# Three latent blocks opened at once with GpSimd's sums of squares put off, and the last retention head's result slots placed behind the sample states

## The chip, the core and the metric

The kernel runs on one core of one Trainium2 chip. A core has five engines with an instruction stream each: TensorE (PE) for matrix products, VectorE (DVE), ScalarE (ACT), GpSimd (POOL) and SyncE (SP), which here mainly issues DMA transfers. On-chip memory is SBUF; matmul results land in PSUM, which is held in banks of 128 x 512 floats. TensorE runs at 1.2 or at 2.4 GHz; the granted clock in the rows is the mean share of the higher level (0.5 is the lower one throughout). The metric is device time in microseconds for one execution; the median of the runs shown is taken.

## What is computed

One step of a decoder layer for a prompt of 512 tokens and, in the same pass, 8 samples of 4 tokens (32 columns), 544 columns in all. Cut from the reference:

```
u = rms_norm(x, p['norm_mix_pre'])
rq, rk, rv, rg, cq, ckv, kpe, xq, gates = split_cols(u @ p['w_in'])
o_ret, ret_state = ret_fn(rope(rq), rope(rk) * RET_DK ** -0.5, rv)    # 4 heads, chunks of 128
o_ret = silu(rg) * (o_ret * rsqrt(mean(o_ret ** 2) + eps));  a_ret = o_ret @ p['w_ret_o']
q = rms_norm(cq) @ p['w_uq'];  ckv = rms_norm(ckv);  kpe = rope(kpe)
a_mla = mla_fn(q, ckv, kpe) ...        # samples: softmax over 2048 paged past positions
a_x = mem_attend(xq, mem_k, mem_v) @ p['w_x_o']
g = sigmoid(gates)                     # 3 x 1024 columns
mixed = g[0] * a_ret + g[1] * a_mla + g[2] * a_x
h = x + rms_norm(mixed @ p['w_out']);  y = h + swiglu_ffn(rms_norm(h))
```

Beside y, the new latents, rotary keys, memory keys and the retention states of prompt (`ret_p`) and samples (`ret_s`) are outputs. The state of a sample is s = s0 * gamma + k v per head; its output takes the state before (s0) and the 4 new tokens.

## The kernel before

Everything is laid out with features on the partitions and the 544 columns along the free axis. A weight product of 128 output features is a *block*: `dense` (L215) goes over two halves of 272 columns and eight chunks k of 128 input features, and because fp32 is split into a high and a low part, it does three matmuls for each (L228 `uh` by `wh`, L229 `ul` by `wh`, L230 `uh` by `wl`): 48 matmuls a block. `uh` and `ul` are the high and low parts of x times the gain. Weights come by SyncE (L199) in tiles `wr`; ScalarE makes `wh` (L207), VectorE or, where it is told so, GpSimd makes `wl` (L208). A ring of 5 `wr`, 5 `wh` and 4 `wl` holds them.

*The start.* A loop over k (L329 to L349) loads x, makes `uh` (L334) and `ul` (L335) on VectorE, squares x on ScalarE (L337, L340) and adds the squares on GpSimd into `xs` (L341). The weights of the first latent blocks (`T_CQ`, `T_CQ+1`, `T_CQ+2`) are asked for in and behind that loop. `latent_project` (L402) then runs the blocks, each with an evacuation by ScalarE (L410, L411) and an add on GpSimd (L414). A block needs two PSUM banks; `mm_tile` hands out three in turn, and `sq_tile` three of another tag. `T_CQ` and `T_CQ+1` have their banks at once. `col_stats` sums `xs` over the features by matmuls with ones (L282, `st`), takes the reciprocal root on VectorE (L245 to L251) and spreads it over the partitions by matmuls (L299, `sb`) into `R1` (L303). `R1` scales each later evacuation of u @ w_in, the rotary ones included.

*Retention* (L659 to L758) runs four heads. Each projects q, k, v, turns them, takes chunk products, builds four chunk states (`pu` L715, `state` L718 and L720, the last stored as `ret_p` by SyncE L722) and outputs (`po` L732, L734), squares them on ScalarE, takes a reciprocal root and scales into `on` (L739), projects the swish gate (two `T_RG` blocks), transposes (`pt` L751) and splits into `oh` and `ol` (L753, L236). In the last head `sample_states` (L623) is called ahead of the chunk states: for four groups of two samples each it loads four states s0 (L634), multiplies them into `poS` (L639), forms key-value products (`km` on GpSimd L647, `puS` L651), updates the state on VectorE (L653) and stores it (L654). The states, the `oh`/`ol` results and gates all take slots of one pool of 41 (`slot`). The last head's `oh` and `ol` slots are taken at its start, three slots `gA` ahead of its chunk products. Then come gate blocks `T_G` and `T_G+1`, `pt`, and `T_G+2`.

*The paged stage* behind it reads pages of past keys and values, by SyncE (L892) and by indirect transfers of GpSimd (L895), for two groups of four samples: key scores `ps_sc` (L903, L910), then value sums `po` (L958) in eight steps a group. Between these, `deal` puts pieces of dense blocks from a list `units` (`w_ret_o` and the remaining gates) by shares worked out from the list's length.

What sets the order: each engine runs its instructions in the order of its own stream, which a tile scheduler made from the program's order and from due times; SyncE's queue blocks behind a transfer that waits. Slots and PSUM banks make later work wait until the earlier reader is done. `together` adds a wait of one instruction for others.

Of the kernel before, what the change touches and what calls it, by code (L numbers as in the profile page):

```python
# [9 lines left out]
F32R = mybir.dt.float32r  # L10
# [4 lines left out]
ALU = mybir.AluOpType  # L15
# [7 lines left out]
RH, DK, DV = 4, 128, 256  # L23
# [134 lines left out]
def step(ctx: ExitStack, tc: tile.TileContext, I, O):  # L158
# [35 lines left out]
    def f32(ap):  # L194
        return ap.bitcast(F32)
# [6 lines left out]
    def wload(src, n, lo=V):  # L202

        raw = wraw(src, n)
        wh = ring.tile([128, 512], F32R, tag="wh", name="wh", bufs=RB[1])[:, :n]
        wl = ring.tile([128, 512], F32R, tag="wl", name="wl", bufs=RB[2])[:, :n]
        S.copy(wh, raw)  # L207
        lo.tensor_tensor(wl, raw, f32(wh), op=ALU.subtract)  # L208
        return wh, wl

    def wk(src, lo=V):

        n = src.shape[1]
        return [(*wload(src[:, c:min(c + 512, n)], min(512, n - c), lo), 0, min(512, n - c) // 128) for c in range(0, n, 512)]
# [51 lines left out]
    def gain(c):  # L266
        return gains[:, c:c + 1]
# [43 lines left out]
    def slot(name, dt=F32):  # L311
        return big.tile([128, NT], dt, tag="big", name=name, bufs=41)
# [5 lines left out]
    def at_tile(name):  # L318
        return at.tile([128, 512], F32, tag="at", name=name, bufs=AB[0])

    def sq_tile(name):
        return at.tile([128, 512], F32, tag="sq", name=name, bufs=SQB[0])

    first = {}

    cqw = []
    uh, ul = [], []
    xs = slot("xs")
    for k in range(8):  # L329
        x = xp.tile([128, NT], F32, tag="x", name="x", bufs=8)  # L330
        SY.dma_start(x, I["xT"][128 * k:128 * k + 128, :])
        h = slot("uh", F32R)
        l = slot("ul", F32R)
        V.tensor_scalar(h, x, gain(G_PRE + k), None, op0=ALU.mult)  # L334
        V.scalar_tensor_tensor(l, x, gain(G_PRE + k), f32(h), op0=ALU.mult, op1=ALU.subtract)  # L335
        if k == 0:
            S.square(xs, x)  # L337
        else:
            sq = xp.tile([128, NT], F32, tag="sq", name="sq", bufs=7)
            S.square(sq, x)  # L340
            G.tensor_tensor(xs, xs, sq, op=ALU.add)  # L341
        uh.append(h)
        ul.append(l)
        if k < 2:
            cqw.append(wload(I["w_in"][T_CQ][:, 512 * k:512 * k + 512], 512))
            first[T_CQ] = [(*w, 0, 4) for w in cqw]
        if k == 3:
            first[T_CQ + 1] = wk(I["w_in"][T_CQ + 1], G)
    SY.dma_start(ident, I["ident"])  # L349
    first[T_CQ + 2] = wk(I["w_in"][T_CQ + 2], G)  # L350
    tabs = latp.tile([128, 2, NT], F32, tag="tabs", name="tabs")
    cosP, sinP = tabs[:, 0, :], tabs[:, 1, :]
    rtab = [slot("rtab") for _ in range(2)]
# [13 lines left out]
    def w_in(t, evac, ps=None):  # L367
        dense(first.pop(t) if t in first else wk(I["w_in"][t]), uh, ul, evac, ps=ps)
# [34 lines left out]
    def latent_project(t0, n):  # L403
        raw, ss = [], slot("lss")
        for i in range(n):
            r_ = slot("lraw")
            sq = ss if i == 0 else slot("lsq")

            def evac(p, s, e):
                S.copy(r_[:, s:e], p)  # L410
                S.square(sq[:, s:e], p)  # L411
            w_in(t0 + i, evac, [sq_tile("mm"), sq_tile("mm")] if t0 + i == T_CQ + 1 else None)
            if i:
                G.tensor_tensor(ss, ss, sq, op=ALU.add)  # L414
            raw.append(r_)
        return raw, ss
# [171 lines left out]
    def gate_evac(dst):  # L588
        def evac(p, s, e):
            z = tmp_tile("gz", "rp_a")[:, :e - s]  # L590
            V.tensor_tensor(z, p, R1[:, s:e], op=ALU.mult)
            S.activation(dst[:, s:e], z, AF.Tanh, scale=0.5)
        return evac

    gA = []
    SH = (1, 2)

    def step_(h):
# [23 lines left out]

    def sample_states():  # L623

        po = at_tile("poS")
        for h in range(RH):
            r = slice(32 * h, 32 * h + 32)
            PE.matmul(po[r, :DV], lhsT=sm[r], rhs=vtS[r], start=True, stop=False, tile_position=(32 * h, 32 * h))
        for b2 in range(DB // 2):
            o = slice(2 * DV * b2, 2 * DV * b2 + 2 * DV)  # L630
            ss, loads = [], []
            for h in range(RH):
                s0 = slot512("s0").rearrange("p (u e) -> p u e", u=2)
                loads.append(SY.dma_start(s0.rearrange("p u e -> p (u e)"), I["s0"][h][:, o]))  # L634
                ss.append(s0)
            for u in range(2):
                b = 2 * b2 + u
                for h in range(RH):
                    lead = PE.matmul(po[32 * h:32 * h + 32, :DV], lhsT=qm[:, h, 32 * b:32 * b + 32], rhs=ss[h][:, u, :],  # L639
                                     start=False, stop=b == DB - 1, tile_position=(0, 32 * h))  # L640
                    if u == 0 and h == 0:
                        together(lead, loads)
            for h in range(RH):
                km = kmp[h]
                if b2 % 2 == 0:
                    km = kmp[h] = slot512("km", F32R)[:96].rearrange("p (b d) -> p b d", b=4)
                    G.tensor_tensor(km, f32(kst[h]).unsqueeze(1).to_broadcast([96, 4, 128]),  # L647
                                    small[:96, C_BM + 2 * b2:C_BM + 2 * b2 + 4].unsqueeze(2).to_broadcast([96, 4, 128]), op=ALU.mult)
                pu = at_tile("puS").rearrange("p (u e) -> p u e", u=2)
                for u in range(2):  # L650
                    PE.matmul(pu[:, u, :], lhsT=km[:, (2 * b2 + u) % 4, :], rhs=vst[h], start=True, stop=True)  # L651
                s0 = ss[h]
                V.scalar_tensor_tensor(s0, s0, GAM4[h], pu, op0=ALU.mult, op1=ALU.add)  # L653
                SY.dma_start(O["ret_s"][h][:, o], s0.rearrange("p u e -> p (u e)"))  # L654
        S.copy(orS, po[:, :DV])
# [1 line left out]
    kmp = [None] * RH  # L657

    for h in range(RH):  # L659
        oh += [slot("oh", F32R) for _ in range(2)]  # L660
        ol += [slot("ol", F32R) for _ in range(2)]
        qT = retp.tile([128, NT], F32, tag="qT", name="qT", bufs=2)
        kT = retp.tile([128, NT], F32, tag="kT", name="kT", bufs=2)
        w_in(T_RQ + h, rope_evac(*rtab, 64, qT))
# [5 lines left out]
            step_(h)  # L670
        if h == 0:
            mstat = memory_prepare()
        if h == RH - 1:
            gA += [slot("gA") for _ in range(3)]


        pst = at_tile("pst").rearrange("p (c i) -> p c i", c=4)
# [26 lines left out]
        kst.append(retp.tile([96, 128], F32R, tag="kst", name="kst", bufs=4))  # L704
        vst.append(retp.tile([96, DV], F32R, tag="vst", name="vst", bufs=4))
        sample_keys(h, px, qT)
        if h == RH - 1:
            sample_states()

        states = []  # L710
        for c2 in range(2):
# [25 lines left out]
        rsqrt(ssq, 4, DV, rr, 4.0)  # L737
        for cc in range(4):
            V.tensor_scalar(on[:, cc, :], pos_[cc // 2][:, cc % 2, :], rr[:, cc:cc + 1], None, op0=ALU.mult)  # L739
        sg = [retp.tile([128, NT], F32, tag="sg", name="sg", bufs=2) for _ in range(2)]  # L740
        for e in range(2):
            w_in(T_RG + 2 * h + e, silu_evac(sg[e]))
# [10 lines left out]
            V.tensor_tensor(og, pt.rearrange("p c i -> p (c i)"), sg[e][:, :NP], op=ALU.mult)  # L753
            split(og, oh[2 * h + e][:, :NP], ol[2 * h + e][:, :NP])
        if h == RH - 1:
            w_in(T_G + 2, gate_evac(gA[2]))
        if h == 1:
            memory_kv(*mstat)  # L758

# [668 lines left out]
```

## Time and profile before

| | us |
|---|---|
| median of three runs | 1243.65 |
| lowest, highest | 1238.79, 1243.99 |
| the profiled execution | 1244.79 |
| its span, first to last instruction | 1243.0 |
| TensorE busy in it | 1184.3 (95%) |
| VectorE, ScalarE, GpSimd busy | 664.0, 450.2, 325.2 |
| mean granted clock | 0.981 |

The profile is one execution. A timeline row has the start, the busy time, the engine, the line, the operation with its output and inputs, a count and, in brackets, the engine's idle time just before and what ended it. Matmuls are pipelined, so one starts before the one ahead of it ends: their rate is read from the starts or from a window's busy time and count. Some matmul records can be missing. The rows on which the prediction rests stand after the change.

### The profile page before, as it was taken

The numbers are of one execution on the slowest core, as the hardware profiler recorded it, in microseconds if no ns is written. First come the engines' busy times: TensorE is split into PE (matmuls) and PEld (weight loads), VectorE is DVE, ScalarE is ACT, GpSimd is POOL, SyncE is SP. The second block draws the span as 40 slices with busy tenths as digits, with TensorE's granted clock in tenths as the row PEclk, the third lists the DMA queues.
The fourth block names the chain that finished last, engine by engine and source line by source line (L and its number), as shares of the span: only waits on it lengthen the run. The fifth ranks groups of instructions, "written<-read, shape, count | busy, mean of one in ns | idle before, by whom it ended". The sixth has DMA issues, their size and how long they took to land.

```text
span 1243.0 us, 24871 instructions
## 1 busy us (share of the span) xinstructions
PE 1184.3 (95%) x9495; PEld 1110.8 (89%) x9495; DVE 664.0 (53%) x1516; ACT 450.2 (36%) x1008; POOL 325.2 (26%) x344
## 2 busy tenths in 40 slices
PE   6999999999799899999899999999999999999996
PEld 6999999978687679789678999999999999999996
DVE  7697574655223223235677859387444544523346
ACT  4334434323122123134446645353333333323341
POOL 6332011211553554400344530034111112100002
PEclk9999999999899899999999999999999999999998
DMA  5332342384686777645121125122222222223343
GB/s 205 98 113 89 123 141 98 104 269 138 200 252 179 228 222 235 203 153 164 37 66 37 47 70 187 52 86 72 85 86 86 94 91 88 86 77 94 94 126 108
DMA packets 87591, 154.87 MB, mean 125 GB/s; under 512 B 11120, under 2 KB 31088, under 8 KB 87472
## 3 DMA queue, kind: packets, MB, share of 16 engines
q1 hardware_dynamic: 73072, 116.57, 29.3%
q0 software_dynamic: 6912, 23.08, 6.2%
q10 hardware_dynamic: 7488, 13.63, 3.4%
q8 instruction: 75, 1.23, 0.4%
q14 instruction: 44, 0.36, 0.1%
HBM read 145.07 MB, written 8.17 MB: 123 GB/s over the span
## 4 chain that ended last, share of the span: by engine, by line
PE 85%; DVE 6%; DMA 4%; issue 3%; ACT 1%; POOL 1%; SPq 0%; DVEq 0%; ACTq 0%; POOLq 0%
PE mm L228 23%; PE mm L229 22%; PE mm L230 22%; PE ps_sc L903 2%; PE po L958 1%; PE pvo L1239 1%; PE pv L1199 1%; PE pk L1184 1%; POOL acc L1128 1%; DMA ret_s<-s 1%; PE ps_sc L910 1%; PE ptm L1232 1%; DMA wr<-w_in 1%; DVE wl L208 1%; DVE ul L335 1%
## 5 line engine op out<-in xcount | busy, mean ns | idle before, releaser
L207 ACT CAST wh<-wr 128x512 fp32r<-128x512 f32 (+2 forms) x316 | 190.6, 605 | 365.8 <-PE mm L229 246.8
L208 DVE TENSOR_TENSOR wl<-wr,wh 128x512 fp32r<-128x512 f32 (+1 forms) x289 | 199.7, 692 | 163.0 <-PE mm L230 104.5
L228 PE MATMUL mm<-uh,wh 128*128 128x272 f32 x896 | 264.9, 297 | 7.9 <-ACT wh L207 5.6
L229 PE MATMUL mm<-ul,wh 128*128 128x272 f32 x896 | 264.1, 295 | 1.9 <-DVE ul L335 1.4
L230 PE MATMUL mm<-uh,wl 128*128 128x272 f32 x896 | 263.2, 294 | 0.4 <-DVE wl L208 0.4
L228 PEld LDWEIGHTS mm<-uh,wh 128*128 128x128 f32 x896 | 170.8, 191 | 13.9 <-ACT wh L207 5.5
L229 PEld LDWEIGHTS mm<-ul,wh 128*128 128x128 f32 x896 | 171.1, 191 | 6.1 <-issue 2.9
L229 PE MATMUL mm<-fl,wh 128*128 128x272 f32 x608 | 175.1, 288 | 0.0
L228 PE MATMUL mm<-fh,wh 128*128 128x272 f32 x608 | 175.0, 288 | 0.0
L230 PEld LDWEIGHTS mm<-uh,wl 128*128 128x128 f32 x896 | 171.3, 191 | 4.0 <-issue 2.9
L230 PE MATMUL mm<-fh,wl 128*128 128x272 f32 x608 | 174.6, 287 | 0.0
L230 PEld LDWEIGHTS mm<-fh,wl 128*128 128x128 f32 x608 | 114.6, 189 | 0.0
L228 PEld LDWEIGHTS mm<-fh,wh 128*128 128x128 f32 x608 | 114.3, 188 | 0.0
L229 PEld LDWEIGHTS mm<-fl,wh 128*128 128x128 f32 x608 | 114.3, 188 | 0.0
L228 PE MATMUL mm<-dh,wh 128*128 128x272 f32 x352 | 101.1, 288 | 0.0
L229 PE MATMUL mm<-dl,wh 128*128 128x272 f32 x352 | 101.1, 288 | 0.0
L230 PE MATMUL mm<-dh,wl 128*128 128x272 f32 x352 | 100.4, 288 | 0.0
L1352 POOL TENSOR_TENSOR m_g<-m_g,R 128x272 f32<-128x272 f32 x44 | 46.1, 1048 | 205.6 <-DVE m_g L1351 194.3
L895 POOL DMA_INDIRECT kt<-kpool,ixk x64 | 61.7, 963 | 85.4 <-DMA kt<-kpool 37.5
L228 PEld LDWEIGHTS mm<-dh,wh 128*128 128x128 f32 x352 | 66.2, 188 | 0.0
L229 PEld LDWEIGHTS mm<-dl,wh 128*128 128x128 f32 x352 | 66.1, 188 | 0.0
L230 PEld LDWEIGHTS mm<-dh,wl 128*128 128x128 f32 x352 | 65.8, 188 | 0.0
(565 smaller groups left out, 2493.8 us busy)
## 6 DMA issues: line engine op xcount, KB each, us to landing
wr<-w_in SPq DMA_DIRECT2D x80, 256.0 KB
wr<-w_fd SPq DMA_DIRECT2D x50, 256.0 KB
wr<-w_fg SPq DMA_DIRECT2D x44, 256.0 KB
wr<-w_fu SPq DMA_DIRECT2D x44, 256.0 KB
kt<-kpool SPq DMA_DIRECT2D x64, 160.0 KB
wr<-w_in ACTq DMA_DIRECT2D x32, 256.0 KB
s<-s SPq DMA_DIRECT2D x16, 256.0 KB
wr<-w_ret_o ACTq DMA_DIRECT2D x16, 256.0 KB
```

The costliest lines, as they stand in the source:

```text
L207: S.copy(wh, raw)
L208: lo.tensor_tensor(wl, raw, f32(wh), op=ALU.subtract)
L228: PE.matmul(p[:, :e - s], lhsT=a, rhs=xh[i][:, s:e], start=i == 0, stop=False)
L229: PE.matmul(p[:, :e - s], lhsT=a, rhs=xl[i][:, s:e], start=False, stop=False)
L230: done.append(PE.matmul(p[:, :e - s], lhsT=b, rhs=xh[i][:, s:e], start=False, stop=i == nk - 1))
L335: V.scalar_tensor_tensor(l, x, gain(G_PRE + k), f32(h), op0=ALU.mult, op1=ALU.subtract)
L895: loads.append(G.indirect_dma_start(k_[:, a, :], None, kflat, bass.IndirectOffsetOnAxis(ixk[:, j:j + 1], 0)))
L903: lead = PE.matmul(o3[rows], lhsT=qlf[i][:, cols], rhs=kt[b][:, :, 128 * i:128 * i + 128].rearrange("p a (j s) -> p a j s", j=2), start=i ...
L910: PE.matmul(o3[rows, :, j, :], lhsT=qzf[j][:, cols], rhs=kt[b][:, :, 256:320], start=False, stop=i == 3)
L958: lead = PE.matmul(po[32 * b:32 * b + 32, :KVL], lhsT=pT[:, 128 * j + 32 * b:128 * j + 32 * b + 32], rhs=vt[b][:, j, :], start=False, stop ...
L1128: G.tensor_tensor(acc[n][:, s:e], acc[n][:, s:e], z, op=ALU.add)
L1352: G.tensor_tensor(g_, g_, R2[:, s:e], op=ALU.mult)
```

## The change

In the start loop ScalarE makes `uh` for six of the eight k, VectorE for k = 3 and 7. All six weight tiles of the three latent blocks are loaded in the loop, for k below 6, with `wl` always on VectorE. The squares move into a second loop, and GpSimd's first add is made to wait for the last `ul`. `T_CQ+2` gets one `sq_tile` and one `mm_tile`, so all three blocks have banks at once. In retention's last head `sample_states` is called behind the scaling into `on`; the head's `oh` and `ol` slots and the `gA` slots are taken behind it. There are four `gA` slots, and `T_G+3` runs in retention behind `T_G+2` and is no longer in the list of the paged stage. `poS` takes a bank of the `sq` tag.

```diff
 for k in range(8):
     x = xp.tile([128, NT], F32, tag="x", name="x", bufs=8)
...
-    V.tensor_scalar(h, x, gain(G_PRE + k), None, op0=ALU.mult)
-    V.scalar_tensor_tensor(l, x, gain(G_PRE + k), f32(h), op0=ALU.mult, op1=ALU.subtract)
-    if k == 0:
-        S.square(xs, x)
-    else:
-        sq = xp.tile([128, NT], F32, tag="sq", name="sq", bufs=7)
-        S.square(sq, x)
-        G.tensor_tensor(xs, xs, sq, op=ALU.add)
+    if k % 4 == 3:
+        V.tensor_scalar(h, x, gain(G_PRE + k), None, op0=ALU.mult)
+    else:
+        S.mul(h, x, gain(G_PRE + k))
+    last = V.scalar_tensor_tensor(l, x, gain(G_PRE + k), f32(h), op0=ALU.mult, op1=ALU.subtract)
...
-    if k < 2:
-        cqw.append(wload(I["w_in"][T_CQ][:, 512 * k:512 * k + 512], 512))
-        first[T_CQ] = [(*w, 0, 4) for w in cqw]
-    if k == 3:
-        first[T_CQ + 1] = wk(I["w_in"][T_CQ + 1], G)
+    if k < 6:
+        t, c = T_CQ + k % 3, 512 * (k // 3)
+        first.setdefault(t, []).append((*wload(I["w_in"][t][:, c:c + 512], 512), 0, 4))
+for k in range(8):
+    if k == 0:
+        S.square(xs, xt_[k])
+    else:
+        sq = xp.tile([128, NT], F32, tag="sq", name="sq", bufs=7)
+        S.square(sq, xt_[k])
+        a = G.tensor_tensor(xs, xs, sq, op=ALU.add)
+        if k == 1:
+            together(a, [last])
-first[T_CQ + 2] = wk(I["w_in"][T_CQ + 2], G)
...
-w_in(t0 + i, evac, [sq_tile("mm"), sq_tile("mm")] if t0 + i == T_CQ + 1 else None)
+w_in(t0 + i, evac, {T_CQ + 1: lambda: [sq_tile("mm"), sq_tile("mm")],
+                    T_CQ + 2: lambda: [sq_tile("mm"), mm_tile("mm")]}.get(t0 + i, lambda: None)())
...
+def head_slots():
+    for o in (oh, ol):
+        o.extend(slot("oh", F32R) for _ in range(2))
...
-    po = at_tile("poS")
+    po = sq_tile("poS")
...
 for h in range(RH):
-    oh += [slot("oh", F32R) for _ in range(2)]
-    ol += [slot("ol", F32R) for _ in range(2)]
+    if h < RH - 1:
+        head_slots()
...
-    if h == RH - 1:
-        gA += [slot("gA") for _ in range(3)]
...
-    if h == RH - 1:
-        sample_states()
...
         V.tensor_scalar(on[:, cc, :], pos_[cc // 2][:, cc % 2, :], rr[:, cc:cc + 1], None, op0=ALU.mult)
+    if h == RH - 1:
+        sample_states()
+        head_slots()
+        gA += [slot("gA") for _ in range(4)]
...
     if h == RH - 1:
-        w_in(T_G + 2, gate_evac(gA[2]))
+        for n in range(2, 4):
+            w_in(T_G + n, gate_evac(gA[n]))
```

On VectorE at the start of the program, before:

```order
L334 TENSOR_SCALAR uh<-x,gains 128x544
L335 SCALAR_TENSOR_TENSOR ul<-x,gains,uh 128x544
L334 TENSOR_SCALAR uh<-x,gains 128x544
L208 TENSOR_TENSOR wl<-wr,wh 128x512
L335 SCALAR_TENSOR_TENSOR ul<-x,gains,uh 128x544
L208 TENSOR_TENSOR wl<-wr,wh 128x512
```

and after:

```order
L338 SCALAR_TENSOR_TENSOR ul<-x,gains,uh 128x544
L208 TENSOR_TENSOR wl<-wr,wh 128x512
L338 SCALAR_TENSOR_TENSOR ul<-x,gains,uh 128x544
L208 TENSOR_TENSOR wl<-wr,wh 128x512
L338 SCALAR_TENSOR_TENSOR ul<-x,gains,uh 128x544
L335 TENSOR_SCALAR uh<-x,gains 128x544
```

Before, each k has a `uh` and a `ul` on VectorE, with `wl` for two of them; now one `uh` in four is left, and a `wl` stands with nearly each `ul`. ScalarE has the other `uh`, the squares and the casts `wh` in turn. TensorE's three blocks have 144 matmuls in both orders; `st` follows the 144th directly before, and behind 62 more after. Between `st` and `sb` stand 43 matmuls before and 10 after.

GpSimd from its first add on, before:

```order
L341 TENSOR_TENSOR xs<-xs,sq 128x544 x3
L208 TENSOR_TENSOR wl<-wr,wh 128x512 x2
L341 TENSOR_TENSOR xs<-xs,sq 128x544
L208 TENSOR_TENSOR wl<-wr,wh 128x512
L341 TENSOR_TENSOR xs<-xs,sq 128x544 x3
```

and after:

```order
L353 TENSOR_TENSOR xs<-xs,sq 128x544 x5
L421 TENSOR_TENSOR lss<-lss,lsq 128x544
L353 TENSOR_TENSOR xs<-xs,sq 128x544
L421 TENSOR_TENSOR lss<-lss,lsq 128x544
L353 TENSOR_TENSOR xs<-xs,sq 128x544
```

The `wl` are gone from GpSimd, and the two adds of the latent squares (`lss`) stand among the last adds of `xs`.

On SyncE in the last head; `s_` with a number is one state tile, four with neighbouring numbers are a group. Before, from the first group's stores to the third group's loads:

```order
L654 DMA ret_s<-s_3118 128x512
L654 DMA ret_s<-s_3120 128x512
L654 DMA ret_s<-s_3122 128x512
L634 DMA s_3198<-s 128x512
L634 DMA s_3200<-s 128x512
L634 DMA s_3202<-s 128x512
L654 DMA ret_s<-s_3124 128x512
L654 DMA ret_s<-s_3162 128x512
L634 DMA s_3204<-s 128x512
```

and after:

```order
L730 DMA ret_p<-state 128x256
L666 DMA ret_s<-s_3162 128x512
L646 DMA s_3242<-s 128x512
L666 DMA ret_s<-s_3164 128x512
L666 DMA ret_s<-s_3166 128x512
L646 DMA s_3244<-s 128x512
L646 DMA s_3246<-s 128x512
L666 DMA ret_s<-s_3168 128x512
L646 DMA s_3248<-s 128x512
```

The head's `ret_p` store, which stood behind all `ret_s` stores, is now ahead of them. The third group's loads (the fourth's follow in the same way) stand among the first group's stores in both. On TensorE 48 instructions stand between the second group's `poS` and the third's before, and `pt` comes right behind `po`; after, `po` stands before most of the sample states, 98 instructions lie between the third and the fourth group, and `T_G+3` stands between `pt` and the first `w_ret_o` block of the last head.

## Rows read from the trace of the kernel before

**Rows 1.** The page, busy time of TensorE, its share and instructions:

```profile
PE 1184.3 (95%) x9495; PEld 1110.8 (89%) x9495; DVE 664.0 (53%) x1516; ACT 450.2 (36%) x1008; POOL 325.2 (26%) x344
```

**Rows 2.** Windows, all engines: us, busy (instructions) by engine, clock, DMA share, GB/s:

```profile
10.00:20.00 10.00, 7.83 (x28) 6.25 (x27) 9.89 (x7) 4.83 (x8) 9.65 (x7) 1.00 0.90 347
```

**Rows 3.** Timeline of VectorE at the start: start, us, line, operation:

```profile
4.17 0.50 DVE L334 TENSOR_SCALAR uh<-x,gains 128x544 fp32r<-128x544 f32 x1 [3.28 <-DMA x<-xT]
4.71 0.78 DVE L335 SCALAR_TENSOR_TENSOR ul<-x,gains,uh 128x544 fp32r<-128x544 f32 x1
...
15.95 1.57 DVE L334 TENSOR_SCALAR uh<-x,gains 128x544 fp32r<-128x544 f32 x1
17.56 1.78 DVE L335 SCALAR_TENSOR_TENSOR ul<-x,gains,uh 128x544 fp32r<-128x544 f32 x1
```

**Rows 4.** Timeline of GpSimd at the start, the adds:

```profile
18.72 5.13 POOL L341 TENSOR_TENSOR xs<-xs,sq 128x544 f32<-128x544 f32 x3
...
31.24 1.36 POOL L414 TENSOR_TENSOR lss<-lss,lsq 128x544 f32<-128x544 f32 x1 [0.74 <-ACT lsq L411]
```

**Rows 5.** Timeline of ScalarE at the start, four squares:

```profile
11.08 2.89 ACT L340 ACTIVATE sq<-x 128x544 f32<-128x544 f32 x4
```

**Rows 6.** Windows of TensorE, tile mm alone: us, busy (records), clock, DMA share, GB/s:

```profile
8.40:16.00 7.60, 5.23 (x17) 1.00 1.05 396
...
24.20:35.18 10.98, 10.98 (x87) 1.00 0.24 73
```

**Rows 7.** Timeline of TensorE at the start:

```profile
16.08 0.59 PE L229 MATMUL mm<-ul,wh 128*128 128x272 f32 x1 [0.89 <-DVE ul L335]
...
20.91 0.43 PE L229 MATMUL mm<-ul,wh 128*128 128x272 f32 x1
21.14 0.34 PE L230 MATMUL mm<-uh,wl 128*128 128x272 f32 x1
21.32 0.29 PE L228 MATMUL mm<-uh,wh 128*128 128x272 f32 x1
...
35.18 1.40 PE L282 MATMUL st<-ones,xs 128*128 128x1 f32 x12
...
41.89 1.41 PE L299 MATMUL sb<-ident,r 128*128 128x128 f32 x12
```

**Rows 8.** Waits of TensorE: waited for, us in total, times, longest:

```profile
PE po L958 <- issue: 3.1, 6, 0.9
...
PE sb L299 <- DVE rs_r L251: 2.5, 1, 2.5
```

**Rows 9.** Timeline of TensorE from the sample states to the paged stage:

```profile
276.95 1.70 PE L639 MATMUL poS<-s,qm 128*32 128x256 f32 x16 [2.41 <-DMA s<-s]
...
298.46 1.61 PE L751 MATMUL pt<-ident,on 128*128 128x128 f32 x8 [1.34 <-DVE on L739]
...
301.47 1.05 PE L228 MATMUL mm<-oh,wh 128*128 128x272 f32 x3 [1.13 <-ACT oh L236]
...
319.67 0.39 PE L229 MATMUL mm<-ol,wh 128*128 128x272 f32 x1 [1.84 <-issue]
```

**Rows 10.** Windows of all engines, from the sample states to the first scores:

```profile
276.00:284.00 8.00, 7.05 (x49) 5.93 (x50) 3.97 (x7) 1.94 (x5) 0.00 (x0) 0.79 0.73 268
300.00:308.00 8.00, 6.87 (x44) 6.58 (x44) 5.28 (x23) 3.21 (x13) 1.69 (x2) 0.79 0.55 150
314.00:330.00 16.00, 10.08 (x70) 7.73 (x70) 2.78 (x5) 1.86 (x3) 7.33 (x8) 0.68 0.53 157
```

**Rows 11.** Chain of waits that ended last, in order of time: start, us, what:

```profile
261.15 5.56 DMA ret_s<-s
...
272.09 4.62 DMA s<-s
```

**Rows 12.** Windows of all engines in the paged stage: keys, then values:

```profile
340.00:390.00 50.00, 49.58 (x496) 44.13 (x496) 17.11 (x35) 14.57 (x25) 20.00 (x21) 1.00 0.70 212
390.00:440.00 50.00, 41.39 (x331) 30.12 (x329) 10.91 (x29) 6.27 (x12) 26.57 (x28) 0.87 0.74 222
```

More of the change, by code (lines that the diff above doesn't have):

```diff
@@ L324, in step @@
     first = {}
-    cqw = []
     uh, ul = [], []
     xs = slot("xs")
+    xt_ = []
     for k in range(8):
@@ L333, in step @@
         l = slot("ul", F32R)
-        V.tensor_scalar(h, x, gain(G_PRE + k), None, op0=ALU.mult)
-        V.scalar_tensor_tensor(l, x, gain(G_PRE + k), f32(h), op0=ALU.mult, op1=ALU.subtract)
+        if k % 4 == 3:
[3 more added lines that the diff above has]
+        last = V.scalar_tensor_tensor(l, x, gain(G_PRE + k), f32(h), op0=ALU.mult, op1=ALU.subtract)
+        xt_.append(x)
+        uh.append(h)
+        ul.append(l)
+        if k < 6:
+            t, c = T_CQ + k % 3, 512 * (k // 3)
+            first.setdefault(t, []).append((*wload(I["w_in"][t][:, c:c + 512], 512), 0, 4))
+    for k in range(8):
         if k == 0:
-            S.square(xs, x)
+            S.square(xs, xt_[k])
         else:
             sq = xp.tile([128, NT], F32, tag="sq", name="sq", bufs=7)
-            S.square(sq, x)
-            G.tensor_tensor(xs, xs, sq, op=ALU.add)
-        uh.append(h)
-        ul.append(l)
-        if k < 2:
-            cqw.append(wload(I["w_in"][T_CQ][:, 512 * k:512 * k + 512], 512))
-            first[T_CQ] = [(*w, 0, 4) for w in cqw]
-        if k == 3:
-            first[T_CQ + 1] = wk(I["w_in"][T_CQ + 1], G)
+            S.square(sq, xt_[k])
+            a = G.tensor_tensor(xs, xs, sq, op=ALU.add)
+            if k == 1:
+                together(a, [last])
     SY.dma_start(ident, I["ident"])
-    first[T_CQ + 2] = wk(I["w_in"][T_CQ + 2], G)
     tabs = latp.tile([128, 2, NT], F32, tag="tabs", name="tabs")
```

## The prediction

> **What bounds the kernel now.** I read the page first: TensorE is busy 1184.3 of 1243.0 us, 95% [rows 1]. An engine that full hides nothing of what it computes, and little is left between its instructions, so only three things can shorten the run: gaps of TensorE, stretches in which it runs at the lower of its two clock levels (1.2 instead of 2.4 GHz), and matmuls taken out. The change takes out none. So I looked for the gaps with the windows, the timelines and the waits of TensorE, at the two places that the diff touches: the first 45 us, and the end of retention with the paged stage behind it.
>
> *The start.* From 10 to 20 us VectorE is busy 9.89 of 10, GpSimd 9.65, TensorE 7.83, ScalarE 4.83 [rows 2]. VectorE bounds it, and the timeline says why: `uh` (L334) and `ul` (L335) take 0.50 and 0.78 us alone, and 1.57 and 1.78 while GpSimd adds squares [rows 3], 3.35 us for one k. Two blocks want 12 matmuls per k. At the low clock one takes about 0.23 us (20.91 to 21.14), so 2.7 us per k: TensorE outruns VectorE and stands, 17 recorded matmuls busy 5.23 of 7.60 us before 16 us [rows 6]. Only at 21.3 us do durations fall from 0.43 and 0.34 to 0.29 us [rows 7]; from 24.20 to 35.18 us 87 matmuls take 10.98 us, 0.126 each [rows 6]. The clock column says 1.00 over all of the start [rows 2, 6]; the durations change as at a rise from the lower level, and I go by them. At 35.18 the three latent blocks (144 matmuls) are done and the column sums `st` begin; their broadcast `sb` follows at 41.89 without a wait [rows 7].
>
> *The sample states.* TensorE stands 2.41 us ahead of the third group's `poS` for state loads, 1.34 ahead of `pt` and 1.13 ahead of the next `w_ret_o` matmul [rows 9]. The two 8 us windows around them have a granted clock of 0.79 [rows 10]. 0.79 is (1 - 0.79) x 2 x 8 = 3.4 us at half clock, half of it lost: 1.7 us each.
>
> *The paged stage.* While keys are read, TensorE is busy 49.58 of 50 us; while values are read, 41.39 [rows 12].
>
> **The change, part by part.** *Start.* Six of eight `uh` leave VectorE for ScalarE, and GpSimd's adds wait for the last `ul`. VectorE's work per k is then 0.50 at most, 0.78, and one `wl` for k below 6. I have no row for `wl` here and take it at no more than the 0.78 of the other two-input operation: under 2.1 us per k against 3.35. ScalarE does 6 `uh`, 8 squares and 7 casts there; its squares take 2.89/4 = 0.72 us [rows 5], so 21 x 0.72 = 15.1 us from 4.2 us on, when the first x has landed [rows 3]: done at 19 us, about 2 us per k. Three blocks open at once want 18 matmuls per k, 18 x 0.23 = 4.1 us at the low clock. That is more than either engine needs for the next k, so TensorE no longer waits once the second k is ready, at 4.2 + 2 x 2.1 = 8.4 us, with 12 matmuls done until then.
>
> When does the clock rise? Before, the last gap of the half-clock stretch ended at 16.1 and the clock rose at 21.3, 5 us later [rows 7]. I take the same 5 us behind 8.4: 13.6, between 11 and 14.4. The Trainium skill (TensorE: Matmul & The Clock Gate, What's actually happening) says that the throttled state is the default and that activity releases it, with a transition point that differs between runs; by it the gapless stretch should raise the clock early, and the trace agrees as far as 5 us after the last gap goes.
>
> Then (13.6 - 8.4)/0.23 = 23 more by 13.6, 35 in all, and the other 109 at 0.126 take 13.7 us: the three blocks end at 27.3 instead of 35.18, a lead of 7.9 us. Not all of it stays. The 7 adds, each 5.13/3 = 1.7 us and two `lss` adds at 1.36 [rows 4], are 14.7 us from the last `ul` (19 us): the sum is ready at 34 to 35 us, as late as `st` is now. TensorE fills until then with the next blocks; the order of the program puts 62 matmuls there, 7.8 us, so it reaches `st` at 35.1 and does not wait for it. But behind `st` only 10 matmuls (1.3 us) stand ahead of `sb`, where 43 stand now, and the reciprocal root on VectorE is longer than that. The nearest row is another `sb`'s wait for the same chain, 2.5 us [rows 8]; I take 2.0 (0 to 2.5). 7.9 - 2.0 = 5.9. The 2.5 itself stands later, in a stretch where VectorE is the late engine; it starts that with the same lead, and I count 0.6 of it as shrinking. **Start: -6.5**, from -3.5 (clock as late as now) to -8.
>
> *Sample states later.* Their matmuls, loads, updates and stores stay as many; they move behind the head's own `pu` and `po`, whose slot pressure and `ret_p` store leave the front of SyncE's queue. What goes is 2.41 + 1.34 + 1.13 = 4.9 us of gaps [rows 9] and two clock drops of 1.7 [rows 10]: -8.3. `pt` no longer follows directly on `po`, and before the new last-head `oh` blocks one more gate stands as cover. What takes their place: the third and fourth groups of state loads still take slots that the stores of the first and second free. The chain shows 5.56 us for such a store and 4.62 for a load [rows 11], 10.2 in a row; in the new order the first update and the third `poS` are 72 matmuls apart, 72 x 0.126 = 9.1 us, so +1.1 and some issue time: +1.5 (0 to 8.3, that is both groups waiting 2.41 with a clock drop of 1.7). GpSimd's `km` and the one `poS` accumulator are moved along and cost nothing as long as TensorE has the `RG` and gate blocks between the groups; without that cover they belong to the same wait. **-6.8**, from 0 to -8.3.
>
> *One gate more in retention, one less in the paged stage.* 48 matmuls x 0.126 = 6.0 us are added ahead of the paged stage and taken out of it. Where keys are read (99% busy) they come back whole; where values are read TensorE has 8.6 us idle per 50 [rows 12] and a filler block taken away is only more idle time. About two thirds of the stage is of the first kind: **+2** (0 to +6).
>
> *The stall at 315 to 323 us.* Between the `w_ret_o` matmuls stand gaps of up to 1.84 us that end with no releaser [rows 9], at a granted clock of 0.68 over 314 to 330 us, in which TensorE is busy 10.08 of 16 [rows 10]. Weights and results are there; I can't name its cause, so I leave it as it is: 0, with -9 as the bound (16 - 10.08 = 5.9 us of idle time, and of 0.32 x 16 = 5.1 us of clock loss the share of busy time, 0.63, 3.2).
>
> Sum: -6.5 - 6.8 + 2 = -11.3 against the profiled 1244.79 us: 1233.5. That execution lies 1.1 us above the median of the runs, 1243.65, so the forecast is **1232.5**.
>
> **Rivals.** A, *the clock rises as late as now*, at 21 us: TensorE starts early but at 0.23 per matmul; the start gives 3.5 instead of 6.5: 1235.5. For it: ScalarE's 15 us leave little room if x lands late (DMA share 0.90 up to 20 us [rows 2]). Against: 18 matmuls per k are more than the supply.
>
> B, *the start does not do what it says*: the adds behind the last `ul` make the first scale factor `R1` later than now, TensorE runs into full accumulators, and 1 us of 6.5 is left: 1238.0. For it: 14.7 us of adds in a chain, and every later evacuation needs `R1`. Against: `st` is at 35.18 already.
>
> C, *the sample-state waits come back*: both later groups wait 2.41 and drop the clock: 8.3 in place of 1.5, so +6.8: 1239.3.
>
> D, *the stall at 315 goes too*, since other work stands there: -9, 1223.5. The rows name no releaser, so neither side has evidence.
>
> E, **slower**: *the paged stage becomes paced by page transfers*. If every one of its 16 value steps then waits the 0.9 us that the longest `po` wait shows now [rows 8], that is 14.4; with the gate's 6.0 not given back, 20.4, less 13.3 = +7.1: 1250.8. It decides once the stage loses more than 13.3 us. For it: DMA is already what TensorE lacks while values are read. Against: six such waits, 3.1 us in all, stand there now [rows 8], and one gate of 24 is a small part of the filler.
>
> **How the numbers follow.** Forecast 0.50, A 0.10, B 0.13, C 0.07, D 0.10, E 0.10. About 0.5%, 6.2 us, is what a measurement of this kernel can tell from no change: 1237.4 and 1249.9 are the bounds. Faster: forecast, A and D, 0.70. Same: B and C, 0.20. Slower: E, 0.10. The range 1222 to 1246 holds all but E and the tails: the forecast with the start at -8 and the sum at -8.3 and no gate cost is 1227, with D 1222 at most of it; the upper end is the start at -3.5, the sample states at 0 and the gate at +6, 1246.
>
> **What would show it.** Start: VectorE's `uh` and `ul` at 0.50 and 0.78, durations at 0.29 us from 14 us on, the third block's last matmul near 27, `st` near 35, `sb` near 39 with a wait of about 2. If `st` comes after 38, B. Sample states: no wait ahead of `pt` and `oh`, at most one ahead of `poS`, granted clock 1.00 from the last head's `pu` to `pt`. Paged stage: 6 us shorter in all if the gate is given back, `po` waits as few as now. It is wrong if the first `ps_sc`, does not come some 7 us earlier than now (6.5 and 6.8 less the 6.0 of the moved gate), or if the stage behind it grows.

## The result and the profile after

The changed kernel takes 1229.22 us (median of 6 runs, 1224.94 to 1232.08) against 1242.16 us for the kernel before in the same series of runs: a ratio of 0.9895 with a 95% interval of 0.9868 to 0.9923, that is -13.0 us (-9.6 to -16.4). Here and below, a difference in us is worked out from such a ratio and the median of the kernel before; the ratio need not be that of the two medians. The forecast was 1232.5 and -11.3. The sum came out right; two of its three terms did not go the way they were told, so that it came out is luck, and most of this part is about that.

The page of the profile after, busy time by engine (compare [rows 1]); the span is 1229.6 us:

```profile
PE 1178.3 (96%) x9495; PEld 1109.7 (90%) x9495; DVE 656.3 (53%) x1514; ACT 452.5 (37%) x1014; POOL 320.0 (26%) x340
```

The start of the kernel after, all engines in windows of 10 us (columns as in [rows 2]):

```profile
10.00:20.00 10.00, 10.00 (x79) 10.00 (x78) 7.30 (x12) 7.95 (x15) 1.02 (x1) 1.00 1.02 388
30.00:40.00 10.00, 8.90 (x67) 8.68 (x66) 3.79 (x15) 3.08 (x8) 5.04 (x6) 0.90 0.43 136
40.00:50.00 10.00, 10.00 (x52) 10.00 (x52) 4.43 (x13) 2.17 (x5) 2.62 (x2) 0.58 0.10 28
```

The timeline of VectorE in it, to hold against [rows 3]:

```profile
8.97 0.69 DVE L208 TENSOR_TENSOR wl<-wr,wh 128x512 fp32r<-128x512 f32 x1 [0.27 <-ACT wh L207]
...
17.01 0.50 DVE L335 TENSOR_SCALAR uh<-x,gains 128x544 fp32r<-128x544 f32 x1
...
18.02 0.78 DVE L338 SCALAR_TENSOR_TENSOR ul<-x,gains,uh 128x544 fp32r<-128x544 f32 x1
22.15 6.94 DVE L208 TENSOR_TENSOR wl<-wr,wh 128x512 fp32r<-128x512 f32 x4 [3.35 <-issue]
```

And that of GpSimd, the first five and the last of the adds (compare [rows 4]):

```profile
18.98 7.80 POOL L353 TENSOR_TENSOR xs<-xs,sq 128x544 f32<-128x544 f32 x5 [17.12 <-DVE ul L338]
...
31.57 1.85 POOL L353 TENSOR_TENSOR xs<-xs,sq 128x544 f32<-128x544 f32 x1
```

From 10 to 20 us TensorE is now busy 10.00 of 10 with 79 recorded matmuls, where it had 7.83 with 28 [rows 2]. `uh` and `ul` take 0.50 and 0.78 us, and ScalarE and VectorE both have time left. The held-back adds run from 18.98 to 33.4 us. Beside them `wl`, 0.69 us at 8.97, takes 6.94/4 = 1.74 from 22.15 us on. The Trainium skill (GPSIMD Engine Reference, 1. Specifications) says that GpSimd shares its SBUF interfaces with VectorE and that instructions with two SBUF inputs contend; `wl` has two, and these rows agree. It cost nothing here, since two `wl` serve 48 matmuls, 6 us.

TensorE at the start, the rise of its clock and the statistics (compare [rows 7]):

```profile
10.05 0.43 PE L229 MATMUL mm<-ul,wh 128*128 128x272 f32 x1
...
11.00 0.29 PE L230 MATMUL mm<-uh,wl 128*128 128x272 f32 x1
...
34.51 1.39 PE L282 MATMUL st<-ones,xs 128*128 128x1 f32 x12
38.38 2.75 PE L299 MATMUL sb<-ident,r 128*128 128x128 f32 x12 [1.10 <-DVE r L251]
```

The matmuls shorten from 0.43 to 0.29 us at 11 us instead of 21.3. `st` comes at 34.51, `sb` at 38.38 after a wait of 1.10 us. But `sb` takes 2.75 us for what took 1.41 [rows 7], and the window from 40 to 50 us has a granted clock of 0.58 and 52 matmuls. Behind the twelve one-column `st` matmuls, ten of full width and the gap, TensorE fell to the lower of its two levels (0.50 from 40 to 48 us).

Waits of TensorE (columns as in [rows 8]):

```profile
PE po L971 <- issue: 7.7, 14, 1.0
...
PE st L282 <- POOL mss L558: 1.7, 1, 1.7
...
PE poS L651 <- DMA s<-s: 0.9, 1, 0.9
```

Of the three gaps of [rows 9], 4.9 us, one of 0.9 is left, ahead of `poS`. The windows of TensorE around the sample states, to hold against [rows 10]:

```profile
278.00:294.00 16.00, 15.12 (x130) 14.31 (x129) 9.13 (x23) 5.41 (x13) 0.00 (x0) 1.00 0.75 246
294.00:310.00 16.00, 16.00 (x131) 15.95 (x130) 9.82 (x36) 6.99 (x20) 2.43 (x3) 1.00 0.49 143
```

No clock drop stands there any more.

Where each part of the run ends, from the profiles (us; first and last `pst`, the chunk products, of the four heads, first `ps_sc`, first `pnM` behind the paged stage, end of the span):

| | pst | last pst | ps_sc | pnM | end |
|---|---|---|---|---|---|
| before | 108.2 | 243.7 | 324.9 | 541.5 | 1243.0 |
| after | 107.4 | 243.0 | 325.2 | 529.8 | 1229.6 |

So in this execution the start gave 0.7 us, the stretch from the last `pst` to the first scores lost 1.0 with a gate's 43 matmuls more in it, the paged stage gave 12.0, and 1.7 came behind it. A single profile almost misleads here, as the experiments show.

### The profile page after: what moved, and what is told of

Read it like the earlier page. It is cut to its first block, busy times and chain, and to the rows that moved or that the text cites. A ratio compares the mean times of both kernels' runs of the same rounds, so it can differ in the third digit from the quotient of the medians.

```text
span 1229.6 us, 24869 instructions
## 1 busy us (share of the span) xinstructions
PE 1178.3 (96%) x9495; PEld 1109.7 (90%) x9495; DVE 656.3 (53%) x1514; ACT 452.5 (37%) x1014; POOL 320.0 (26%) x340
## 4 chain that ended last, share of the span: by engine, by line
PE 86%; DVE 5%; DMA 4%; issue 3%; ACT 2%; POOL 0%; SPq 0%; DVEq 0%; ACTq 0%; POOLq 0%
PE mm L228 23%; PE mm L229 23%; PE mm L230 23%; PE po L971 2%; PE ps_sc L916 1%; PE pvo L1252 1%; DMA wr<-w_in 1%; PE pv L1212 1%; PE pk L1197 1%; PE ps_sc L923 1%; PE sb L299 1%; DVE wl L208 1%; PE ptm L1245 1%; PE st L282 1%; PE pu L723 1%
## 5 line engine op out<-in xcount | busy, mean ns | idle before, releaser
L208 DVE TENSOR_TENSOR wl<-wr,wh 128x512 fp32r<-128x512 f32 (+2 forms) x293 | 206.6, 707 | 155.5 <-PE mm L230 97.6
```

## The experiments

Time times mean granted clock is given beside some medians: it is about the time at the full clock, and it takes out the clock drops, which fall differently in each execution. That they go with the time can be read from the runs of one kernel: the changed kernel's six in one series go from 1208.37 us at a mean clock of 0.984 to 1201.01 at 0.993. Times the clock these two are 1189.0 and 1192.6, so for a single run the measure is good to some 4 us only.

**One part each.** The start alone, that is the changed kernel with retention as before:

```diff
-        if h == RH - 1:
-            sample_states()
-            head_slots()
-            gA += [slot("gA") for _ in range(4)]
...
-            for n in range(2, 4):
-                w_in(T_G + n, gate_evac(gA[n]))
+            w_in(T_G + 2, gate_evac(gA[2]))
```

> Only the start of the change (uh on ScalarE, weights in the loop, GpSimd's adds behind the last ul, banks for three blocks); retention and the paged stage as before. My prediction gave this part -6.5 us. The rival, read from the trace of the changed kernel: the lead of about 6 us is given back by a clock drop from sb on (38 to 49 us at half clock, 5 us) and in VectorE's full stretch from 50 to 100 us, so that the first pst of head 0 comes at 107 against 108 us and the whole is 0 to -2 us.

> The start alone, again, beside the retention part alone. If the start gives what its lead at head 0 is (5.0 us without a clock drop, 0.7 with one), the median is -2 to -5 against before. My prediction had -6.5.

Measured: 1237.74 against 1246.70 us, 0.9921 (0.9895 to 0.9947), -9.8 us; and in a second series, on another chip, 1240.61 against 1243.76, 0.9966 (0.9943 to 0.9989), -4.2 us. Times the clock it is 1215.2 and 1214.1 against 1220.3 and 1220.6: -5 and -6.5. The rival's "0 to -2" fell in the first series, and with it my reading of the changed kernel's profile; the second's interval (-1.4 to -7.1) touches it.

The row of `pst` (first and last start) in the kernel after:

```profile
L689 PE MATMUL pst<-qT,kT x32: 271/275/275, 107.4 to 243.0; 128*128 128x128 f32 x32
```

and in the start alone, the same program up to there:

```profile
L686 PE MATMUL pst<-qT,kT x32: 271/275/275, 103.2 to 238.8; 128*128 128x128 f32 x32
```

The windows of all engines around `sb` and behind the memory's `st`, in the kernel after:

```profile
38.00:49.00 11.00, 10.62 (x50) 10.63 (x51) 3.90 (x12) 1.17 (x3) 2.62 (x2) 0.53 0.07 16
97.00:103.00 6.00, 5.37 (x31) 5.37 (x32) 4.71 (x17) 1.89 (x4) 0.79 (x2) 0.72 0.39 128
```

and in the start alone:

```profile
38.00:49.00 11.00, 10.17 (x83) 10.17 (x84) 8.06 (x22) 2.64 (x7) 5.01 (x3) 1.00 0.23 65
97.00:103.00 6.00, 6.00 (x50) 6.00 (x50) 5.57 (x20) 1.46 (x3) 0.99 (x2) 1.00 0.28 87
```

In this profile of the start alone the clock stayed at 1.00 in both places, and every `pst` is 4.2 us earlier than in the kernel after, 5.0 than before. Its second profile, r_e1, has a short drop there:

```profile
38.00:49.00 11.00, 11.00 (x79) 11.00 (x79) 7.87 (x21) 2.21 (x5) 4.49 (x3) 0.84 0.16 49
```

So the drop differs between executions of the same start. Of the six profiles with it, after, e3 and r_after have a granted clock of 0.53 from 38 to 49 us and the last `pst` at 243.0 to 243.6 us; r_e1 has 0.84 and 239.1; e1 and e8 have 1.00 and 238.8 and 238.2. The drop goes with the time at which the clock first rose, the first matmul of 0.29 us: 9.79 us in r_e1, 10.92 to 11.41 in the three with the long drop, 12.08 and 12.51 in the two without; e5 (below), 9.95, has 0.84 like r_e1. That one sets the other is not shown. The two profiles of before have the last `pst` at 243.7 and 245.2, and 1.00 from 38 to 49 us.

The retention part alone, the changed kernel with the start (loop, weights, banks) as before:

```diff
-        if k % 4 == 3:
-            V.tensor_scalar(h, x, gain(G_PRE + k), None, op0=ALU.mult)
-        else:
-            S.mul(h, x, gain(G_PRE + k))
+        V.tensor_scalar(h, x, gain(G_PRE + k), None, op0=ALU.mult)
...
-            if k == 1:
-                together(a, [last])
...
+    first[T_CQ + 2] = wk(I["w_in"][T_CQ + 2], G)
```

> Only the retention part (sample states, slots, four gates, poS bank); the start as before. My prediction gave -6.8 + 2 = -4.8 us. The rival, from the trace of the changed kernel: retention gives about 5 us and the moved gate is given back whole and more in the paged stage, together -11 to -13 us. By the rival the first ps_sc comes within 1 us of before (324.9), by the prediction not more than 1 us earlier either; they part behind it: the stretch from the first ps_sc to pnM is 216.6 us before, by the rival 205, by the prediction 212.

> The retention part alone. On a chip without the gaps of the paged stage only the waits ahead of poS, pt and oh and their clock drops can go, and the gate that moves is cost and gain at once: -5 to -8 against before. My prediction had -4.8 (6.8 less 2).

Measured: 1240.63 against 1246.70, 0.9943 (0.9926 to 0.9960), -7.1 us; again 1238.20 against 1243.76, 0.9956 (0.9937 to 0.9975), -5.5 us. From the first `ps_sc` to `pnM` the two profiles take 206.8 and 211.1 us, one near either expectation. The second chip did have the gaps of the paged stage (17.0 us), so that premise fell. Times the clock the retention part gives only -0.8 and -2.5: its gain is for the most part in clock drops that are gone. Parts and whole agree within their intervals: -7.0 and -6.3 in the mean of two series, -13.3 together, against -13.0.

**The gate.** The changed kernel with `T_G+3` back in the list of the paged stage:

```diff
-gA += [slot("gA") for _ in range(4)]
+gA += [slot("gA") for _ in range(3)]
-            for n in range(2, 4):
+            for n in range(2, 3):
                 w_in(T_G + n, gate_evac(gA[n]))
```

> The changed kernel with three gA slots, T_G+3 back in the list of the paged stage. By my prediction (a gate moved out of the paged stage is given back only in its key phases) this is 2 us faster than the changed kernel, about -15 against before. If the gate is given back whole: equal to the changed kernel, -13, with first ps_sc 6 us earlier and the paged stage 6 us longer. If a shorter list helps the paged stage beyond its matmuls: 3 to 6 us slower than the changed kernel.

Measured: 1242.38 against 1246.70, 0.9962 (0.9940 to 0.9984), -4.7 us: some 8 us slower than the changed kernel by the ratios (two series; beside it e6, the changed kernel with its adds on VectorE, has 0.9889). The third of the expectations held, more than in its size. The reason is in the key phases, each from a group's first `ps_sc` to its first `ps_new`, the scores of the new tokens. The windows of the two key phases hold TensorE's matmuls of the dense blocks alone (us, busy, recorded count, clock, DMA). In the kernel before:

```profile
324.91:376.11 51.20, 34.95 (x260) 0.97 0.77 235
431.43:489.54 58.11, 38.19 (x283) 0.97 0.75 242
```

In the kernel after:

```profile
325.18:375.83 50.65, 35.28 (x265) 0.97 0.80 243
431.99:480.40 48.41, 32.67 (x240) 1.00 0.79 242
```

With the gate back:

```profile
324.36:374.38 50.02, 30.38 (x221) 0.96 0.79 230
428.85:488.40 59.55, 39.10 (x283) 0.94 0.76 238
```

The first key phase takes 50 to 51 us with 260, 265 or 221 matmuls: its length does not follow them. The second takes 58 to 60 us with 283 and 48 with 240. With the gate back, as many matmuls of the dense blocks run ahead of the first `ps_sc` as without it (1796 and 1800 recorded, 1757 before): list blocks take the gate's place. They come out of the first phase, where they cost nothing, and the second keeps its 283. The gate in retention shortens the list, `deal` spreads it thinner, and 43 matmuls leave the second phase.

All ten profiles from the chips with a before of 1242 to 1247 us say so. From the last `pst` to `pnM`, and the second key phase with its recorded matmuls:

| | gate | last `pst` to `pnM`, us | second key phase, us (matmuls) |
|---|---|---|---|
| before, r_before | in the list | 297.8, 296.2 | 58.1, 58.0 (283) |
| e1, r_e1: start alone | in the list | 295.9, 296.8 | 59.6, 59.5 (283) |
| e3: gate back | in the list | 295.7 | 59.6 (283) |
| after, e2, r_e2, e6, e10 | in retention | 286.8, 289.3, 287.5, 287.7, 289.8 | 48.4, 50.7, 48.9, 48.8, 48.9 (240) |

43 matmuls at 0.126 are 5.4 us of some 9.5. The phase's clock, 0.94 to 0.97 with the longer list and 1.00 with the shorter, and gaps of TensorE without a releaser, 2.7 to 4.1 us in its first 10 us against 0.9 to 1.9, go the same way.

The table holds a second result. e3 has the late slots and none of the three gaps of [rows 9], and yet takes almost as long from `pst` to `pnM` as the kernels with the old retention; its median is no better than that of the start alone (-4.7 us, and -9.8 and -4.2; times the clock 1215.5, and 1215.2 in the same series). Without the gate's move, the late slots gained little or nothing that these runs show. Whether the gate needs the room that they make was not tried.

That the first phase's length does not follow its matmuls holds on these chips. On the faster chip (below) r_after has TensorE busy all through it:

```profile
316.43:362.68 46.25, 46.22 (x522) 40.86 (x521) 14.73 (x26) 10.90 (x20) 32.97 (x34) 1.00 0.94 303
```

No run there has the gate back.

**The place of the sample states.** Called where they stood before, with the slots taken late and four gates:

```diff
         sample_keys(h, px, qT)
+        if h == RH - 1:
+            sample_states()
...
-            sample_states()
             head_slots()
             gA += [slot("gA") for _ in range(4)]
```

> The changed kernel with sample_states called where it stood before, the result and gate slots still taken late, four gates. If the place of the sample states is what takes the gaps away (my prediction, 8.3 us with the two clock drops): gaps of 2 us ahead of poS and over 1 ahead of pt or oh, granted clock 0.8 around them, 5 to 8 us slower than the changed kernel. If the slots kept late and the fourth gate do it: equal to the changed kernel within 2 us.

> The changed kernel once more, in the same call as the three below. If the clock drop behind sb (38 to 49 us) comes in some executions only, as it did in the changed kernel and not in the kernel with the start alone (same program up to there), its profile shows either pst of head 0 near 107 with the drop or near 103 without; if it belongs to the program, near 107 again. Median -11 to -14 against before.

Measured in one series on a faster chip (before 1213.66): r_after 1204.35, 0.9921 (0.9897 to 0.9945); e8 1203.65, 0.9925 (0.9897 to 0.9953). Equal. The waits of e8 that answer to [rows 9]:

```profile
PE mm L229 <- DVE oh L237: 0.7, 2, 0.4
PE mm L228 <- ACT oh L236: 0.5, 1, 0.5
PE poS L651 <- DMA ret_s<-s: 0.3, 1, 0.3
```

With the slots kept late, 0.3 us is left ahead of `poS` even in the old place, where the start alone, with early slots, has 3.2 and 2.8. So the slots take away this wait. They do not take that for `oh`: 1.2 us in the start alone, 0.7 + 0.5 in e8, none in r_after; and `pt` has no wait in the start alone already. From the last `pst` to the first `ps_sc` e8 takes 73.7 us and r_after 72.8, to `pnM` 257.3 and 259.2: the move of the sample states is worth nothing that these runs show. That e1 ran on another chip keeps the part of the slots from being shown in full.

**Holding the adds back.**

```diff
             a = G.tensor_tensor(xs, xs, sq, op=ALU.add)
-            if k == 1:
-                together(a, [last])
```

> The changed kernel without the wait of GpSimd's first add for the last ul, so the adds run beside uh, ul and wl again. If holding them back is what frees VectorE: its two-input operations are stretched from 0.7 and 0.8 to 1.7 us again, 8 ul and 6 wl or 14 us more, TensorE has gaps before 25 us, the clock rises later, and pst of head 0 comes 3 to 5 us later than without a drop (103); total +3 to +5 against the changed kernel. If moving uh to ScalarE and opening three blocks is enough, TensorE has no gap behind 9 us and the total is equal within 1 us.

Measured: 1204.61, 0.9922 (0.9894 to 0.9949), equal to r_after. The timeline of GpSimd without the wait, its first adds:

```profile
17.63 8.26 POOL L353 TENSOR_TENSOR xs<-xs,sq 128x544 f32<-128x544 f32 x5 [15.78 <-ACT xs L349]
```

and VectorE's last `ul` there:

```profile
17.48 0.78 DVE L338 SCALAR_TENSOR_TENSOR ul<-x,gains,uh 128x544 fp32r<-128x544 f32 x1
```

The first add comes at 17.63 instead of 18.98 and waits for ScalarE's square of the first x, `xs`, which is the last of ScalarE's squares in the order. Its place in the order holds the adds back without `together`; the last `ul` is at 17.48. This wait shows no effect of its own, and the experiment doesn't tell what adds beside `ul` would cost in the new start.

**The adds on VectorE**, so that `st` comes earlier and 44 rows stand between `st` and `sb`:

```diff
-            a = G.tensor_tensor(xs, xs, sq, op=ALU.add)
-            if k == 1:
-                together(a, [last])
+            V.tensor_tensor(xs, xs, sq, op=ALU.add)
```

> The changed kernel with the adds of the squares on VectorE instead of GpSimd, and no wait for the last ul. In its order st comes after about 140 rows instead of 190 and 44 rows stand between st and sb instead of 11. If the clock drop behind sb is what takes the lead: granted clock 1.00 from 30 to 50 us, st near 27, pst of head 0 3 to 5 us earlier than in the changed kernel, total -3 to -5 against it. If VectorE's full stretch from 50 to 100 us takes whatever lead there is: no clock drop, yet pst of head 0 within 1 us of 107 and the total equal.

Measured: 1233.92 against 1246.70, 0.9889 (0.9855 to 0.9923), -13.8 us: not to be told from the changed kernel. The start did what was expected: `st` at 28.7, no clock drop from 38 to 49 us, last `pst` at 238.4. A second one stands further on, where TensorE waits 2.8 us for `mss`, the squares of the memory tokens, as its windows show:

```profile
38.00:49.00 11.00, 11.00 (x91) 11.00 (x90) 8.07 (x22) 3.14 (x7) 4.04 (x3) 1.00 0.27 96
90.00:100.00 10.00, 7.19 (x46) 6.97 (x45) 7.80 (x27) 2.61 (x6) 1.37 (x4) 0.83 0.29 89
```

So, on top of that edit, the memory's `st` was put behind head 0 (e9), and then half of `mn` moved from VectorE to ScalarE too (e10):

```diff
-        return mrb, col_stats(at, [mss], ((0, NM),), D, mrb)[0]
+        return mrb, mss
...
+        if h == 0:
+            mstat = mstat[0], col_stats(at, [mstat[1]], ((0, NM),), D, mstat[0])[0]
```

```diff
-            V.tensor_scalar(hl[:, 0], m_[:, :NM], gain(G_MEM + k), None, op0=ALU.mult)
+            S.mul(hl[:, 0], m_[:, :NM], gain(G_MEM + k))
```

> The changed kernel with the adds of the squares on VectorE (as before in this study) and the column sums of the memory tokens (st from mss) at the end of head 0 instead of ahead of its pst, where TensorE waited 1.1 to 2.8 us for GpSimd and the granted clock fell to 0.64 or 0.83 behind it. If that wait and drop are a cost of TensorE: no wait for mss, clock 1.00 from 90 to 110 us, pst of head 0 at 98 to 100, total 3 to 4 us below the changed kernel. If VectorE holds TensorE up there anyway, the gap turns up at another instruction and the total is equal.

> The kernel with the squares' adds on VectorE and the memory statistics later, and besides the eight mn multiplications of the memory tokens on ScalarE instead of VectorE (2.7 us of VectorE's work between 83 and 100 us). If VectorE holds TensorE in that stretch, the last pst comes 1 to 3 us earlier than 235.2 and the median is 1 to 3 us below the changed kernel's; if not, equal.

Measured: e9 1204.96, 0.9929 (0.9904 to 0.9955) beside r_after's 0.9921 in the same series; e10, with both edits, 1230.46 against 1243.76, 0.9887 (0.9858 to 0.9917). Both lose the wait and the drop, and the last `pst` comes at 235.2 and 234.1 us, 8 and 10 us before r_after's 243.6. The medians don't show it: neither is shown to beat the changed kernel. Where that lead goes in the other executions stays open; r_after's profile is the slowest of its six runs and e9's the fastest, so the two profiles overstate it.

**The gaps without a releaser.**

> The kernel before once more, for its profile beside the next three on the same chip. If the gaps without a releaser in the paged stage belong to the chip of the first runs, there are none here, the first ps_sc comes at 316 to 318 us and the stretch from it to pnM is near 190; if they belong to the program, about 20 us of them stand there as in the first profile.

Measured: one run, 1247.20 us, 17.8 us of such gaps between 230 and 560 us, 20.0 in the first profile of before. All ten profiles from chips with a before of 1242 to 1247 us have 16 to 25 us of them, most in the same places of the program. The four profiled on the chip with a before of 1213.66 have 0.2 to 3.4. The window of [rows 10] in r_after:

```profile
314.00:330.00 16.00, 15.97 (x185) 14.06 (x185) 4.67 (x8) 2.47 (x5) 12.32 (x13) 1.00 0.96 310
```

TensorE is busy 15.97 of 16 at the full clock where before had 10.08 at 0.68, and from the first `ps_sc` to `pnM` r_after takes 186.4 us, the same program on the other chip 204.6. The gaps belong to the chip or its surroundings, not to the program alone: `pnM` is 27 us earlier in this profile, the end of the span 23. What makes them stays open. The change gains there too, -9.6 us (-6.7 to -12.5).

## Why the sum was right and its terms were not

By the sign that the prediction itself gave, its account was wrong: the first `ps_sc` should come some 7 us earlier, and in the profile after it comes at 325.2 us instead of 324.9. The `po` waits did not stay as few either.

**The start, -6.5.** Right in size: -9.8 and -4.2 alone, -5 to -6.5 at full clock. Its steps: TensorE has no gap behind 7 us (forecast 8.4); the clock rose at 11.0 (13.6); the last block's evacuation is at 27.4 (27.3); `st` 34.51 (35.1); the wait at `sb` 1.1 (2.0). The 0.6 us that I counted as shrinking had no ground: the row of 2.5 us [rows 8] has no time, and it stands at the end of the run, 2.52 us before and 2.51 after, not in a stretch behind the start:

```profile
1232.68 1.16 PE L299 MATMUL sb<-ident,rs_r 128*128 128x128 f32 x6 [2.52 <-DVE rs_r L251]
```

How much of the lead is kept without the clock drop can be read from ScalarE's copies of `sb` into `lrb` (first and last start). Before:

```profile
L303 ACT COPY lrb<-sb x2: 387/387/387, 60.4 to 81.8; 128x272 f32<-128x272 f32 x2
```

and in the start alone:

```profile
L303 ACT COPY lrb<-sb x2: 386/386/386, 51.5 to 75.9; 128x272 f32<-128x272 f32 x2
```

That is 8.9 us at the first and 5.9 at the second. But the first copy stands behind 303 recorded matmuls of the dense blocks before and 284 now, and 19 x 0.126 = 2.4 us of the 8.9 are that; at the second it is 442 and 443. So the lead is 6.5, then 5.9, then 5.0 at `pst`, ahead of which TensorE waits 2.3 us for `mss` instead of 1.1: about what was forecast. What I did not put in is the clock drop behind `sb`, which takes 4 to 5 us of it in three of the six profiles with this start: I saw the 10 matmuls between `st` and `sb`, priced the wait and not the clock. The trace of before showed the price twice, in [rows 10]: a gap of 1 to 2.4 us, then 1.7 us lost. Rival A (a late clock) and B (`R1` late) are out: `st` and the clock were both early. B's size, 1 us of 6.5 left, is near the 0.7 of the profile after, for another reason.

**Sample states, -6.8.** The gaps went as told, 4.9 to about 1.5 us, and both clock drops. From the last `pst` to the first `ps_sc` it is 82.2 us instead of 81.2 with 43 matmuls more, 43 x 0.126 = 5.4: -4.4 in this pair of profiles. As a saving of its own the term failed: in e3 the gaps are gone too, list blocks fill the room, they leave a first key phase that does not get shorter, and the time stays that of the start alone. The stall at 315 us, 5.2 us of gaps instead of 5.9, was rightly left in. The cause was only half right: I put the gaps down to the place of the sample states, and e8 says that for `poS` the late slots suffice. Of C one wait came back, 0.9 us, without a clock drop.

**The gate, +2.** The step that failed most. It said that the gate comes back whole where keys are read, two thirds of it overall. In fact the cost ahead, 5.4 us, was taken by the retention's gaps, and the paged stage became 12.0 us shorter, not 4: 43 matmuls left the second key phase, which is 9.7 us shorter. Putting the gate back costs some 8 us. I took two phases with TensorE 99% busy for alike; in the first one, on these chips, more or fewer filler matmuls fit into the same 50 us. What sets that length is not shown. Which phase loses a filler is decided by `deal`, and I had not counted the filler of each phase in the two orders, though that could be read beforehand.

Rival E (paged stage slower) had the sign of one row right: the `po` waits grew from 3.1 us in 6 to 7.7 in 14, but they have no releaser, so they do not show page transfers, and the stage as a whole got shorter. Rival D's stall went only on another chip. The errors offset: in the profiled execution the start gave 5.8 too little, the states 2.4 too little, the gate and the paged stage 8.6 more than told (-6.6 for +2), and 1.7 came behind it, where nothing was changed: -0.7 - 4.4 - 6.6 - 1.7 = -13.4, the difference of the two spans. That they offset to within 2 us of the forecast is luck.

## What to carry to other kernels

A filler is worth what its phase is worth: count, phase by phase, how many filler matmuls the program's order holds before and after, and look for a phase whose length doesn't change with that number. A gap taken away ahead of such a phase may be worth nothing by itself. Between a reduction on TensorE and its broadcast leave full-width matmuls enough for the chain on the other engine; a wait of 1 us there may cost several in clock, in some executions and not in others. So judge a change of 1% by medians and by time times granted clock, and use a profile for where things stand, not for how much a part gives.

## What the runs showed of the hardware

- The fall of the clock differs between executions: the same instructions around `sb` ran at 1.00, 0.84 or 0.53 (38 to 49 us), with the last `pst` 4 to 5 us later at 0.53. With 43 full-width matmuls between `st` and `sb` in place of ten, all seven profiles (before, r_before, e2, r_e2, e6, e9, e10) have 1.00 there. The rise came between 9.79 and 12.51 us in the six profiles of the new start, with the first matmul at 6.67 to 6.76 in all. The Trainium skill (TensorE: Matmul & The Clock Gate, What's actually happening) says of the rise that its point varies by half a microsecond either way and depends on where the activity falls; these profiles agree that it varies, by more than that, 2.7 us. The fall varies in them too.
- Gaps of TensorE without a releaser, 16 to 25 us a run, stand on some chips and are almost absent (0.2 to 3.4 us) on another, where the same kernel is 2% faster.
- VectorE's `wl`, 0.69 us alone, took 1.74 beside GpSimd's adds, the mean of four. One that began just ahead of an add, at 31.52 us, kept its 0.69; that add took 1.85 us.
